# Both layers' attention of a two-layer diffusion backbone: one score buffer, one maximum and one exponential per head

## The chip, the cores and the metric

The kernel runs on one core of one Trainium2 chip. The metric is the device time of one execution in microseconds (us). Engines are named as in the profile: PE (TensorE matmul), PEld (its weight loads), DVE (VectorE), ACT (ScalarE), POOL (GpSimd), SP (SyncE, which issues most transfers).

## What is computed

Two layers over 1024 latent tokens and 256 context tokens, width 1024. Each layer mixes tokens (attention beside a gating or convolution branch), then sends them through 16 experts that choose their tokens by top-k. The change lies in the two attentions. Layer 0 has windows of 128 queries, each over up to 384 nearby keys and 256 context keys, 8 heads, with a sink; layer 1 is dense over 1024 + 256 = 1280 keys, 8 heads:

```python
def gqa_attend(q, k, v, mask, sink, scale):
    s = jnp.einsum('bqhgd,bkhd->bhgqk', q, k).astype(jnp.float32) * scale
    if mask is not None:
        s = jnp.where(mask, s, NEG_INF)
    if sink is not None:
        sk = jnp.broadcast_to(sink.astype(jnp.float32)[None, :, :, None, None], s.shape[:-1] + (1,))
        s = jnp.concatenate([s, sk], axis=-1)
    p = jax.nn.softmax(s, axis=-1)
    ...
    return jnp.einsum('bhgqk,bkhd->bqhgd', p.astype(v.dtype), v)

def dense_block_attention(q, k_all, v_all, scale):
    ...
    def block(nidx):
        qb = lax.dynamic_slice_in_dim(q, nidx * C_BLOCK, C_BLOCK, axis=1)
        return gqa_attend(qb[:, :, :, None], k_all, v_all, None, None, scale)[:, :, :, 0]
```

## The kernel before, in words

All matmuls take fp16 operands split into a high and a low part, so that a product is three matmuls (`mm3`, L141 to L143). Splitting a tile costs an ACT copy for the high part (L112) and a DVE subtraction for the low part (L114). Transposes of fp16 tiles go through DMA, issued on SP (`turn`, L147).

Work is written as streams (Python generators) that `weave` interleaves by weights. The scheduler of the framework then orders the instructions of each engine by priority, and each engine runs its list in that order. Attention's stream has a raised priority.

Layer 0 (`even`): 10 tiles of 128 tokens (2 context, 8 latent). `score(keep, u)` (L769) handles one latent head, or two context heads. It writes two score tiles `sps` of one PSUM bank each (up to 384 window keys, and 256 context keys; four banks in all, `MB[2]` = 4), takes the maximum of each (L791) and folds it into the negative maximum `negm` (L792), runs one exponential per head and block with its row sum (L799), splits the result and transposes it. `values()` multiplies with V one or two units later. The score of unit u+2 is written ahead of the values of unit u.

Layer 1 (`odd`): 8 tiles of 128 queries by 8 heads, in one sequence of 64 heads. `score(t, h, i)` (L1192) handles one of three key chunks of a head (`KB`: 512, 512 and 256 keys) in a score tile `sps1` of one bank, five banks in all (`AB[4]` = 5). Three matmuls per chunk (L1201) and one maximum (L1202). After the third chunk come the joint maximum (L1208), its scaling (L1209), three exponentials with row sums (L1218, each followed by a read of the accumulator), three splits into `ps1`, two DMA transposes (8 and 12 blocks of 128 columns, as high and low parts count apart) into `pT1`, and the sum of the three row sums (L1230). Scores run `LA` = 3 heads ahead of `values()`; `SP` says which chunks of head n+3 are scored with which of head n's value steps. Two of the eight banks serve the convolution and the projections (`zc`, `zt`), one the output accumulator `po1`.

Beside attention two streams fill PE in layer 1. First `conv_all` (576 matmuls of 512 columns into `cvps`), after which the output weights are scaled (`wraw`, L1159) and split (`owo`). Then `tails`: per tile 48 matmuls of the output projection (`yps`), a residual addition (`xx`, L301), router logits and affinities `aff` (L334). A top-k over the first 640 tokens (`tkvr`, L350 to L354) needs the first five tiles, a second over the other 384 (`tkvl`) the rest; then the expert stage starts and fills the remaining 596 us.

Of the kernel before, what the change touches and what calls it, by code (L numbers as in the profile page):

```python
# [47 lines left out]
GR = ((0,), (1, 2))  # L48
# [29 lines left out]
class Net:  # L78
# [554 lines left out]
    def even(self, xd, xdc, h2d, h2dc, then):  # L633
        nc, tc, V, S, T, G, Y, I = self.nc, self.tc, self.V, self.S, self.T, self.G, self.Y, self.I
        with self.pool("m0") as pm, self.pool("m0p", PSUM) as pp:
# [133 lines left out]
            def score(keep, u):  # L769

                qT, blocks, masks, W, nh = keep["q"], keep["blocks"], keep["masks"], keep["W"], keep["nh"]
                if u == 0:
                    keep["negm"] = self.small.tile([P, 8], F32, name="negm", bufs=2)
                    keep["den"] = self.small.tile([P, 8, 2], F32, name="den", bufs=2)
                    if len(blocks) == 1:
                        V.memset(keep["den"], 0.0)
                negm, hs = keep["negm"], slice(u * nh, u * nh + nh)
                pss, lim = [], nsink[:, hs]
                for first, n in blocks:
                    ps = pp.tile([P, 512], F32, name="sps", tag="s", bufs=MB[2])  # L780
                    pss.append(ps)
                    sl = slice(first * P, (first + n) * P)
                    for i in range(nh):
                        h, o = u * nh + i, ps[:, i * n * P:(i + 1) * n * P]
                        mk = masks if first == blocks[0][0] else []
                        T.matmul(o, qT[:, 0, h], kT[:, h // 4, sl], start=True, stop=False)
# [3 lines left out]
                    mx = self.small.tile([P, 2], F32, name="mx", bufs=4)  # L790
# [4 lines left out]
                c0 = 0  # L795
                for i in range(nh):
                    h = u * nh + i
                    for j, (_, n) in enumerate(blocks):
                        S.activation(pr[:, c0:c0 + n * P], pss[j][:, i * n * P:(i + 1) * n * P], AF.Exp, bias=negm[:, h:h + 1], scale=SC0,  # L799
                                     accum_out=keep["den"][:, h, j:j + 1])  # L800
                        c0 += n * P
# [7 lines left out]
            def values():  # L809
# [17 lines left out]
                V.tensor_tensor(es, den[:, :, 0], es, OP.add)  # L827
                V.tensor_tensor(es, den[:, :, 1], es, OP.add)
# [152 lines left out]
    def odd(self, ms, mw, xs, xsc, xd, h2d, W, then):  # L981
# [9 lines left out]
        if True:  # L991
# [109 lines left out]
            KB = ((0, 512), (512, 512), (1024, 256))  # L1101
            SP = ((), (0, 1), (2,))
# [6 lines left out]
            with self.pool("m1zp", PSUM) as pz:  # L1109
# [57 lines left out]
                if True:  # L1167
                    def Q(t):
                        qT = []
                        for i in range(2):  # L1170
# [5 lines left out]
                            S.activation(q, z, AF.Copy, scale=IS)  # L1176
# [14 lines left out]

                    def score(t, h, i):  # L1192

                        qT, (c0, w) = K[t][h // 4], KB[i]
                        if i == 0:
                            K["mx"] = self.small.tile([P, 3], F32, name="mx3", bufs=3)
                            K["sp"] = []
                        mx, sp = K["mx"], K["sp"]
                        ps = pp.tile([P, 512], F32, name="sps1", tag="s", bufs=AB[4])
# [6 lines left out]
                        dn = self.small.tile([P, 3], F32, name="dn3", bufs=3)  # L1206
                        nm = self.small.tile([P, 1], F32, name="nm1", bufs=3)
                        V.tensor_reduce(nm, mx, axis=AX.X, op=OP.max)  # L1208
                        V.tensor_scalar(nm, nm, -SC1, None, op0=OP.mult)  # L1209
                        pTs = []  # L1210
                        for g, parts in enumerate(GR):
                            n = sum(KB[i][1] for i in parts)
                            ps = pt1.tile([P, 2, n], F16, name="ps1", tag=f"ps{g}", bufs=AB[1])
                            o = 0
                            for i in parts:
                                w = KB[i][1]
                                pr = pt1.tile([P, 512], F32, name="pr1", bufs=AB[0])
                                S.activation(pr[:, :w], sp[i][:, :w], AF.Exp, bias=nm, scale=SC1, accum_out=dn[:, i:i + 1])  # L1218
                                self.split_a(pr[:, :w], ps[:, 0, o:o + w], ps[:, 1, o:o + w])
                                o += w  # L1220
                            pT = pt1.tile([P, 2, n // P, P], F16, name="pT1", tag=f"pT{g}", bufs=AB[2])
                            self.turn(pT.rearrange("p s b c -> p (s b) c"), ps.rearrange("p s c -> p (s c)"))
                            o = 0
                            for i in parts:
# [257 lines left out]
```

## Time and profile before

| | us |
|---|---|
| runs of the kernel, median of 3 (lowest to highest) | 2640.53 (2639.13 to 2646.84) |
| profiled execution, its own time | 2632.11 |
| span of its profile, first to last instruction | 2630.0 |
| busy in the span: PE / DVE / ACT | 2329.2 / 1997.7 / 1696.7 |
| layer 1's attention: first score matmul | 1503.4 |
| last convolution matmul | 1724.3 |
| last value matmul | 1937.20 |
| last output projection matmul | 1972.50 |
| mean granted TensorE clock (1.00 is 2.4 GHz) | 0.943 |

Times inside the program are counted from the first instruction of the profiled execution. Matmuls overlap in PE's pipeline, so a busy PE in a table of stretches need not be a full one; the distance between the starts of successive matmuls tells what one costs.

### The profile page before, as it was taken

Reading aid. Unit: us, or ns where it says so; the run is one execution under the profiler, and the core shown is the slowest. Engines: PE = TensorE matmul, PEld = TensorE weight load, DVE = VectorE, ACT = ScalarE, POOL = GpSimd, SP = SyncE. Lnnn points to the kernel's source line nnn. Section 1 sums busy time; section 2 is a strip of 40 time slices with the busy share of each in tenths; the row PEclk is TensorE's granted clock in tenths of the full one; section 3 lists DMA queues with packets and bytes.
Section 4 is the critical chain, followed back from the end, with each engine's and each line's share of the span. In section 5 each row is a group of like instructions: output and inputs, shape, how many; then the busy total and the mean of one; then the engine's idle time right before and its main releaser. Section 6 shows DMA issues by size and latency. Waiting matters only on the chain. (4 is left out here: it accounts for less than half of the span.)

```text
span 2630.0 us, 48132 instructions
## 1 busy us (share of the span) xinstructions
PE 2329.2 (89%) x19023; PEld 1415.0 (54%) x19023; DVE 1997.7 (76%) x3586; ACT 1696.7 (65%) x2748; POOL 320.6 (12%) x196
## 2 busy tenths in 40 slices
PE   6889998867999999999969999978982999999995
PEld 2335555543877778786836555535541444444442
DVE  5546767787887788777848687788796889888887
ACT  4434666535777787777726466567655777777774
POOL 1000000003111111111310000000025011112120
PEclk9999999877999999999989999989985999999998
DMA  8783555548998989888967577788866899999997
GB/s 321 192 213 84 134 104 116 123 126 312 352 337 324 328 328 325 327 320 300 326 187 203 119 143 143 133 151 184 176 175 272 311 364 395 368 360 367 361 363 274
DMA packets 461705, 660.25 MB, mean 251 GB/s; under 512 B 371083, under 2 KB 371387, under 8 KB 410789
## 3 DMA queue, kind: packets, MB, share of 16 engines
q1 hardware_dynamic: 439894, 582.81, 69.7%
q0 software_dynamic: 21584, 74.37, 9.8%
q8 instruction: 149, 2.44, 0.4%
q14 instruction: 78, 0.64, 0.1%
HBM read 525.82 MB, written 41.94 MB: 216 GB/s over the span
## 5 line engine op out<-in xcount | busy, mean ns | idle before, releaser
L101 DVE SCALAR_TENSOR_TENSOR spl<-raw,spl 128x2048 f16<-128x2048 f32 x369 | 834.6, 2285 | 167.3 <-ACT spl L100 166.5
L100 ACT ACTIVATE spl<-raw 128x2048 f16<-128x2048 f32 x369 | 693.5, 1911 | 166.4 <-DMA raw<-in_w 109.5
L141 PE MATMUL pa<-xsh,spl 128*128 128x160 f16 x1024 | 214.6, 233 | 2.3 <-ACT xsh L112 2.3
L143 PE MATMUL pb<-xsh,spl 128*128 128x160 f16 x1024 | 214.6, 233 | 0.5 <-DVE spl L101 0.5
L142 PE MATMUL pa<-xsl,spl 128*128 128x160 f16 x1024 | 214.7, 233 | 0.3 <-DVE xsl L114 0.3
L143 PE MATMUL pa<-xsh,spl 128*128 128x160 f16 x1024 | 214.7, 233 | 0.0
L142 PE MATMUL pb<-xsl,spl 128*128 128x160 f16 x1024 | 214.6, 233 | 0.0
L141 PE MATMUL pb<-xsh,spl 128*128 128x160 f16 x1024 | 214.5, 233 | 0.0
L141 PEld LDWEIGHTS <-spl 128*128 128x128 f16 x2048 | 200.6, 98 | 8.9 <-issue 8.0
L141 PE MATMUL y<-spl,gh 128*128 128x512 f16 x512 | 195.2, 384 | 9.0 <-ACT gh L112 8.4
L143 PEld LDWEIGHTS <-spl 128*128 128x128 f16 x2048 | 200.8, 98 | 1.1 <-DVE spl L101 0.7
L142 PEld LDWEIGHTS <-spl 128*128 128x128 f16 x2048 | 200.8, 98 | 0.3
L143 PE MATMUL y<-spl,gl 128*128 128x512 f16 x512 | 190.1, 386 | 11.4 <-DVE gl L114 11.3
L142 PE MATMUL y<-spl,gh 128*128 128x512 f16 x512 | 195.6, 382 | 1.8 <-DVE spl L101 1.8
L594 POOL DMA_INDIRECT xd<-ysb,idxl x31 | 113.2, 3652 | 532.3 <-DVE ysb L587 508.2
L1218 ACT ACTIVATE pr<-sps,nm 128x512 f32<-128x512 f32 (+1 forms) x192 | 116.7, 611 | 88.3 <-DVE nm L1209 67.7
L141 PE MATMUL po<-vS,pT 128*128 128x64 f16 x976 | 118.0, 198 | 49.1 <-DMA pT<-ps 32.5
L1201 PE MATMUL sps<-kT,qT 128*128 128x512 f16 (+1 forms) x576 | 134.4, 355 | 12.3 <-ACT pr L1218 11.9
L114 DVE TENSOR_TENSOR ps<-pr,ps 128x512 f16<-128x512 f32 (+1 forms) x192 | 112.2, 595 | 38.9 <-ACT ps L112 38.3
L141 PEld LDWEIGHTS <-pT 128*128 128x128 f16 x976 | 92.1, 101 | 82.8 <-DMA pT<-ps 46.5
L1202 DVE TENSOR_REDUCE mx<-sps 128x1 f32<-128x512 f32 (+1 forms) x192 | 112.8, 595 | 26.2 <-PE sps L1201 24.9
L208 PE MATMUL modps<-mslab,cs 128*2 128x512 f32 x384 | 88.5, 690 | 33.6 <-DMA mslab<-in_mod_w 28.7
(431 smaller groups left out, 5883.8 us busy)
## 6 DMA issues: line engine op xcount, KB each, us to landing
raw<-in_w SPq DMA_DIRECT2D x384, 1024.0 KB, 6.8
mslab<-in_mod_w SPq DMA_DIRECT2D x80, 512.0 KB, 4.8
mslab<-in_mod_w SPq DMA_DIRECT2D x8, 1024.0 KB, 8.2
raw<-in_wz SPq DMA_DIRECT2D x12, 512.0 KB, 6.4
raw<-in_wconv SPq DMA_DIRECT2D x24, 256.0 KB, 3.8
xin<-in_x POOLq DMA_DIRECT2D x8, 512.0 KB, 4.8
raw<-in_ev_wo SPq DMA_DIRECT2D x8, 512.0 KB, 6.9
xres<-in_x POOLq DMA_DIRECT2D x8, 512.0 KB, 5.4
```

Source lines behind the costliest of these rows:

```text
L100: self.S.activation(hi, raw, AF.Copy, scale=scale)
L101: self.V.scalar_tensor_tensor(lo, raw, scale, hi, op0=OP.mult, op1=OP.subtract)
L114: return self.V.tensor_tensor(lo, src, hi, OP.subtract)
L141: self.T.matmul(ps, lh, rh, start=first, stop=False)
L142: self.T.matmul(ps, lh, rl, start=False, stop=False)
L143: return self.T.matmul(ps, ll, rh, start=False, stop=last).ins
L208: T.matmul(ps[c0:c0 + 2], lhs, slab[:rows, g * 512:(g + 1) * 512], start=False, stop=(k == 8), tile_position=(0, c0))
L594: G.indirect_dma_start(out=xd, out_offset=IOA(ap=lat[0][:, e:e + 1], axis=0), in_=ysb, in_offset=None, compute_op=OP.add)
L1201: T.matmul(ps[:, :w], qT[:, 4 * j + h % 4], kT[:, k, c0:c0 + w], start=j == 0, stop=j == 2)
L1202: V.tensor_reduce(mx[:, i:i + 1], ps[:, :w], axis=AX.X, op=OP.max)
L1218: S.activation(pr[:, :w], sp[i][:, :w], AF.Exp, bias=nm, scale=SC1, accum_out=dn[:, i:i + 1])
```

## The change

In layer 0 a unit's blocks now lie side by side in one tile of two banks (two such tiles), placed so that the boundary between blocks falls on the bank boundary. One maximum, one folding step, and one exponential per head over all its keys (640 or 512) remain; the row sum needs no addition of two parts.

In layer 1 one tile `two` of five banks holds two heads, 1280 columns each, used in turn. The chunks of the odd half are 256, 512 and 512 keys so that each stays within a bank. One maximum (negated), one exponential over 1280 keys with the whole row sum, one split, and two transposes of 10 blocks each remain. The scale `SC1` moves into the copy of q. The buffer `pr1` of the exponentials is one tile of 1280 (before, two of 512).

```diff
-                for first, n in blocks:
-                    ps = pp.tile([P, 512], F32, name="sps", tag="s", bufs=MB[2])
...
+                ps = pp.tile([P, 1024], F32, name="sps", tag="s", bufs=MB[2] // 2)
+                base = 512 - blocks[0][1] * P if len(blocks) > 1 else 0
...
-                    V.tensor_reduce(mx[:, :nh], ps[:, :nh * n * P].rearrange("p (h w) -> p h w", h=nh), axis=AX.X, op=OP.max)
-                    V.scalar_tensor_tensor(negm[:, hs], mx[:, :nh], -SC0, lim, op0=OP.mult, op1=OP.min)
-                    lim = negm[:, hs]
+                V.tensor_reduce(mx[:, :nh], ps[:, base:base + nh * W].rearrange("p (h w) -> p h w", h=nh), axis=AX.X, op=OP.max)
+                V.scalar_tensor_tensor(negm[:, hs], mx[:, :nh], -SC0, nsink[:, hs], op0=OP.mult, op1=OP.min)
...
+                    S.activation(pr[:, i * W:i * W + W], ps[:, base + i * W:base + i * W + W], AF.Exp, bias=negm[:, h:h + 1], scale=SC0,
+                                 accum_out=keep["den"][:, h:h + 1])
...
-            KB = ((0, 512), (512, 512), (1024, 256))
-            SP = ((), (0, 1), (2,))
+            KB = ((0, 512), (512, 512), (1024, 256)), ((0, 256), (256, 512), (768, 512))
+            SP = (0, 1), (2,)
...
-                            S.activation(q, z, AF.Copy, scale=IS)
+                            S.activation(q, z, AF.Copy, scale=IS * SC1)
...
+                    two = pp.tile([P, 2560], F32, name="sps1")
+
                     def score(t, h, i):
...
+                        n = (8 * t + h) % 2
+                        qT, (c0, w) = K[t][h // 4], KB[n][i]
+                        ps = two[:, 1280 * n:1280 * n + 1280]
                         for j, k in enumerate((h, h, 8)):
-                            T.matmul(ps[:, :w], qT[:, 4 * j + h % 4], kT[:, k, c0:c0 + w], start=j == 0, stop=j == 2)
-                        V.tensor_reduce(mx[:, i:i + 1], ps[:, :w], axis=AX.X, op=OP.max)
-                        sp.append(ps)
-                        if i < len(KB) - 1:
+                            T.matmul(ps[:, c0:c0 + w], qT[:, 4 * j + h % 4], kT[:, k, c0:c0 + w], start=j == 0, stop=j == 2)
+                        if i < len(KB[n]) - 1:
                             return
...
+                        V.tensor_reduce(nm, ps, axis=AX.X, op=OP.max, negate=True)
...
+                        pr = pt1.tile([P, 1280], F32, name="pr1", bufs=1)
+                        S.activation(pr, ps, AF.Exp, bias=nm, accum_out=K["rd", t][:, h:h + 1])
+                        pf = pt1.tile([P, 2, 2, 640], F16, name="ps1", bufs=AB[1])
+                        prg = pr.rearrange("p (g c) -> p g c", g=2)
+                        self.split_a(prg, pf[:, :, 0], pf[:, :, 1])
...
-                        for b in range(w // P):
-                            vb, vs = c0 // P + b, slice(h * 64, h * 64 + 64)
+                        for b in range(5):
+                            vb, vs = 5 * i + b, slice(h * 64, h * 64 + 64)
```

How the order of instructions moves is shown at three places. The first is PE's list at layer 1's second head (`sps` is a score tile, `kT` and `qT` the keys and queries, `wc` convolution weights; a wait names the engine whose semaphore it awaits). Before, the head's first two chunks:

```order
L1201 LDWEIGHTS qT_18993
L1201 MATMUL sps_19060<-kT_16901,qT_18993 128x512
L1201 LDWEIGHTS qT_18993
L1201 MATMUL sps_19060<-kT_16901,qT_18993 128x512
L1201 LDWEIGHTS qT_18993
L1201 MATMUL sps_19060<-kT_16901,qT_18993 128x512
L1201 LDWEIGHTS qT_18993
L1201 MATMUL sps_19065<-kT_16901,qT_18993 128x512
L1201 LDWEIGHTS qT_18993
L1201 MATMUL sps_19065<-kT_16901,qT_18993 128x512
```

Of the change, the same head's first chunk, with the convolution ahead of it:

```order
L141 LDWEIGHTS wc
L141 MATMUL cvps<-hTl,wc 128x512
L142 LDWEIGHTS wc
L142 MATMUL cvps<-hTl,wc 128x512
L1193 LDWEIGHTS qT_18662
L1193 MATMUL sps_18639<-kT_16569,qT_18662 128x256 [waits Activation_49]
L1193 LDWEIGHTS qT_18662
L1193 MATMUL sps_18639<-kT_16569,qT_18662 128x256
```

The chunks had tiles of their own and no wait; now every head's matmuls name one tile, and the head's first one waits for ACT.

The second place is DVE's list near the end of layer 1's attention (`mx` and `nm` come from the maximum over scores, `ps<-pr` is the subtraction that gives the low part). Before:

```order
L1202 TENSOR_REDUCE mx_24516<-sps_24517 128x1
L114 TENSOR_TENSOR ps_24473<-pr_24474,ps_24473 128x512
L1202 TENSOR_REDUCE mx_24516<-sps_24522 128x1
L1202 TENSOR_REDUCE mx_24516<-sps_24545 128x1
L114 TENSOR_TENSOR ps_24480<-pr_24481,ps_24480 128x512
L1202 TENSOR_REDUCE mx_24606<-sps_24607 128x1
L1208 TENSOR_REDUCE nm_24551<-mx_24516 128x1
L1230 TENSOR_REDUCE rd<-dn_24469 128x1
L1249 TENSOR_TENSOR oc<-po_23773,rd 128x512
L114 TENSOR_TENSOR ps_24480<-pr_24485,ps_24480 128x256
```

Of the change, four heads there:

```order
L113 TENSOR_TENSOR ps_22944<-pr_22942,ps_22944 128x2x640
L1197 TENSOR_REDUCE nm_22990<-sps_18639 128x1
L113 TENSOR_TENSOR ps_22994<-pr_22992,ps_22994 128x2x640
L1197 TENSOR_REDUCE nm_23049<-sps_18639 128x1
L113 TENSOR_TENSOR ps_23053<-pr_23051,ps_23053 128x2x640
L1197 TENSOR_REDUCE nm_23099<-sps_18639 128x1
```

Chunks of neighbouring heads stood mixed; now a head's subtraction and the next head's maximum alternate strictly.

The third place is DVE's list where the first top-k of layer 1 stands (`tkvr`, `tkir`; `oc` is the last step of the attention of a tile, here of the last one). Before, in the midst of that top-k:

```order
L354 MATCH_REPLACE aff<-tkvr,aff 16x640
L350 MAX tkvr<-aff 16x8
L1249 TENSOR_TENSOR oc<-po_24593,rd 128x512
L352 MAX_INDEX tkir<-tkvr,aff 16x8
L114 TENSOR_TENSOR oh<-oc,oh 128x512
L354 MATCH_REPLACE aff<-tkvr,aff 16x640
```

Of the change, the start of that top-k, 26 rows behind the last `oc`:

```order
L126 TENSOR_SCALAR rstdt<-rstt,rsyt 128x1
L300 SCALAR_TENSOR_TENSOR xx<-yps,xx 128x512
L333 COPY aff<-affps 16x128
L349 MAX tkvr<-aff 16x8
L351 MAX_INDEX tkir<-tkvr,aff 16x8
L353 MATCH_REPLACE aff<-tkvr,aff 16x640
```

It had begun before the attention ended; now it begins after the fifth tile's affinities, which come behind the attention.

## Rows read from the trace of the kernel before

**Rows 1.** Stretches of layer 1: length, PE, PEld, DVE, ACT, POOL busy, clock, DMA.

```profile
1503.00:1725.00 222.00, 215.69 (x1850) 118.25 (x1849) 168.75 (x424) 140.72 (x351) 0.00 (x0) 1.00 0.73 136
1725.00:1784.00 59.00, 38.70 (x381) 21.22 (x379) 52.76 (x113) 42.03 (x95) 0.00 (x0) 0.80 0.81 172
1784.00:1855.00 71.00, 62.81 (x603) 37.10 (x599) 54.95 (x153) 49.12 (x122) 2.14 (x4) 1.00 0.89 170
1855.00:1918.00 63.00, 58.96 (x574) 36.22 (x574) 46.46 (x133) 44.62 (x112) 2.66 (x5) 1.00 0.87 178
1918.00:1937.00 19.00, 10.79 (x142) 8.16 (x142) 16.87 (x46) 10.50 (x28) 0.53 (x1) 0.72 1.00 188
1937.00:1973.00 36.00, 36.00 (x184) 18.08 (x182) 35.04 (x87) 20.46 (x19) 17.56 (x7) 0.96 0.45 171
```

**Rows 2.** Groups by line and shape, 1500 to 1940 us: count, busy us, mean ns, idle before.

```profile
L1202 DVE TENSOR_REDUCE mx<-sps 128x1 f32<-128x512 f32 x128 | 87.2, 684 | 15.6 <-PE sps L1201 14.6
L1218 ACT ACTIVATE pr<-sps,nm 128x512 f32<-128x512 f32 x128 | 86.5, 680 | 70.0 <-DVE nm L1209 67.7 <-DVE ps L114 2.0
L114 DVE TENSOR_TENSOR ps<-pr,ps 128x512 f16<-128x512 f32 x128 | 85.7, 684 | 35.9 <-ACT ps L112 35.6
...
L112 ACT ACTIVATE ps<-pr 128x512 f16<-128x512 f32 x128 | 75.1, 625 | 0.3
...
L1218 ACT ACTIVATION_READ_ACCUMULATOR pr<-sps,nm 128x1 f32 x192 | 37.6, 196 | 0.0
...
L1218 ACT ACTIVATE pr<-sps,nm 128x256 f32<-128x256 f32 x64 | 30.1, 471 | 18.3 <-DVE ps L114 18.3
L1202 DVE TENSOR_REDUCE mx<-sps 128x1 f32<-128x256 f32 x64 | 26.7, 417 | 10.6 <-PE sps L1201 10.3
L114 DVE TENSOR_TENSOR ps<-pr,ps 128x256 f16<-128x256 f32 x64 | 26.6, 416 | 3.0 <-ACT ps L112 2.7
L112 ACT ACTIVATE ps<-pr 128x256 f16<-128x256 f32 x64 | 26.6, 415 | 1.7
...
L1159 DVE TENSOR_TENSOR wraw<-wraw,m2b 128x1024 f32<-128x1024 f32 x8 | 9.5, 1215 | 1.2 <-DMA wraw<-in_od_wo 1.2
...
L101 DVE SCALAR_TENSOR_TENSOR owo<-wraw,owo 128x1024 f16<-128x1024 f32 x8 | 9.4, 1208 | 0.0
```

**Rows 3.** PE's timeline: start us, duration us; value matmuls, then convolution matmuls.

```profile
1517.16 0.19 PE L142 MATMUL po<-vS,pT 128*128 128x64 f16 x1
1517.19 0.19 PE L143 MATMUL po<-vS,pT 128*128 128x64 f16 x1
...
1625.45 0.38 PE L141 MATMUL cvps<-hTl,wc 128*128 128x512 f16 x1
1625.67 0.38 PE L142 MATMUL cvps<-hTl,wc 128*128 128x512 f16 x1
```

**Rows 4.** Layer 0: PE's wait, 190 to 400 us; exponentials, 190 to 570 us.

```profile
PE sps L786 <- ACT pr L799: 7.6, 5, 3.1
...
L799 ACT ACTIVATE pr<-sps,negm 128x256 f32<-128x256 f32 x80 | 37.1, 467 | 7.7 <-DVE negm L792 6.1 <-DVE p L114 1.6
...
L799 ACT ACTIVATE pr<-sps,negm 128x384 f32<-128x384 f32 x48 | 27.5, 574 | 12.0 <-DVE negm L792 7.1 <-DVE p L114 4.8
```

**Rows 5.** Timelines of DVE and of ACT: one handover between them.

```profile
1625.73 0.14 DVE L1209 TENSOR_SCALAR nm<-nm 128x1 f32<-128x1 f32 x1
...
1625.91 0.69 ACT L1218 ACTIVATE pr<-sps,nm 128x512 f32<-128x512 f32 x1 [1.68 <-DVE nm L1209]
```

**Rows 6.** Transposes into `pT1`, 1500 to 1940 us, from issue to landing.

```profile
DMA to landing us min/median/max: 3.0/3.7/6.3
```

**Rows 7.** DVE's timeline: the first top-k's first and last step, the second's first.

```profile
1925.35 0.82 DVE L350 MAX8 tkvr<-aff 16x8 f32<-16x640 f32 x1
...
1974.39 0.23 DVE L360 TENSOR_SCALAR tkir<-tkir 16x128 f32<-16x128 uint32 x1
...
1997.64 0.55 DVE L350 MAX8 tkvl<-aff 16x8 f32<-16x384 f32 x1
```

More of the change, by code (lines that the diff above doesn't have):

```diff
@@ L773, in score @@
                     keep["negm"] = self.small.tile([P, 8], F32, name="negm", bufs=2)
-                    keep["den"] = self.small.tile([P, 8, 2], F32, name="den", bufs=2)
-                    if len(blocks) == 1:
-                        V.memset(keep["den"], 0.0)
+                    keep["den"] = self.small.tile([P, 8], F32, name="den", bufs=2)
                 negm, hs = keep["negm"], slice(u * nh, u * nh + nh)
-                pss, lim = [], nsink[:, hs]
-                for first, n in blocks:
-                    ps = pp.tile([P, 512], F32, name="sps", tag="s", bufs=MB[2])
[L781 to L784, printed above, removed]
+                ps = pp.tile([P, 1024], F32, name="sps", tag="s", bufs=MB[2] // 2)
+                base = 512 - blocks[0][1] * P if len(blocks) > 1 else 0
+                for i in range(nh):
+                    h, c0 = u * nh + i, base + i * W
+                    for first, n in blocks:
+                        o = ps[:, c0:c0 + n * P]
+                        c0 += n * P
                         mk = masks if first == blocks[0][0] else []
+                        sl = slice(first * P, (first + n) * P)
                         T.matmul(o, qT[:, 0, h], kT[:, h // 4, sl], start=True, stop=False)
@@ L789, in score @@
                             T.matmul(o[:, c:c + P], identb, maskb[:, w], start=False, stop=j == len(mk) - 1)
[L790 to L793 removed]
+                mx = self.small.tile([P, 2], F32, name="mx", bufs=4)
+                V.tensor_reduce(mx[:, :nh], ps[:, base:base + nh * W].rearrange("p (h w) -> p h w", h=nh), axis=AX.X, op=OP.max)
+                V.scalar_tensor_tensor(negm[:, hs], mx[:, :nh], -SC0, nsink[:, hs], op0=OP.mult, op1=OP.min)
                 pr = pm.tile([P, 640], F32, name="pr", bufs=MB[3])
[L795 removed]
                 for i in range(nh):
                     h = u * nh + i
[L798 to L801, printed above, removed]
+                    S.activation(pr[:, i * W:i * W + W], ps[:, base + i * W:base + i * W + W], AF.Exp, bias=negm[:, h:h + 1], scale=SC0,
+                                 accum_out=keep["den"][:, h:h + 1])
                 n = nh * W
@@ L1205, in score @@
                             return
-                        dn = self.small.tile([P, 3], F32, name="dn3", bufs=3)
                         nm = self.small.tile([P, 1], F32, name="nm1", bufs=3)
[L1208 to L1224, printed above, removed]
-                                w = KB[i][1] // P
-                                pTs.append(pT[:, :, o:o + w])
-                                o += w
@@ L1231, in score @@
+                        prg = pr.rearrange("p (g c) -> p g c", g=2)
+                        self.split_a(prg, pf[:, :, 0], pf[:, :, 1])
+                        pTs = []
+                        for g in range(2):
+                            pT = pt1.tile([P, 2, 5, P], F16, name="pT1", tag=f"pT{g}", bufs=AB[2])
+                            self.turn(pT.rearrange("p s b c -> p (s b) c"), pf[:, g].rearrange("p s c -> p (s c)"))
+                            pTs.append(pT)
                         K["p", t, h] = pTs
@@ L1261, in att_all @@
                             pTs = K.pop(("p", t, h))
-                            for i in range(len(KB)):
+                            for i in range(2):
                                 pend.append((t, h, i, pTs[i]))
```

14 lines of the change are left out of this document (2 added, 12 removed).

## The prediction

> **What bounds the kernel now.** I read first the busy time by stretch of layer 1's attention [rows 1], since most of the change lies there, and then what each of its instructions costs [rows 2]. Call a head's pieces S (9 score matmuls), M (maximum), E (exponential), C (high part, ScalarE), D (low part, VectorE), T (two DMA transposes) and V (30 value matmuls). In the first stretch, 222 us for heads 0 to 33, PE is busy 215.69 us at clock 1.00. That it is also full follows from spacing: 512-column matmuls start 0.215 us apart and value matmuls 0.03 us [rows 3]. So S takes 6 x 0.215 + 3 x 0.11 = 1.6 us, V 0.9, nine projections of q (384 columns) 1.45. By the built order this stretch holds 552 convolution matmuls (118.7 us), 34 heads of S and V (85) and 14 such projections (20): 224 us. Nothing taken from VectorE or ScalarE shortens it. In the second stretch (59 us, heads 33 to 42) PE is busy 38.70 us at clock 0.80 and VectorE 52.76: VectorE paces it. In the third and fourth (heads 42 to 63) PE is at 62.81 of 71 and 58.96 of 63, because output projections fill it; then the last heads drain until 1937, where the last value matmul stands, and the three remaining output tiles take 36 us, 12 us each. Layer 0 is close to PE-bound too; what the scores there wait for is the exponential of an earlier head, 7.6 us in five waits between 190 and 400 us [rows 4].
>
> **What the change saves.** Per element and fixed part follow from the two widths of [rows 2]. M: 684 and 417 ns, so 1280 keys take 684 + 768 x 1.043 = 1.49 us where 2 x 684 + 417 = 1.79 stood. D: 684 and 416, the same, 1.49. E: 680 and 471, so 1.31 us where 1.83 stood. C: 625 and 415, so 1.26 where 1.67 stood. An accumulator read costs 196 ns and two of three go. Over 64 heads VectorE loses 38 us in M and D and some 28 us in three small instructions a head, taken at 0.145 us like the one of the three in [rows 5], ScalarE 33 + 26 + 25 = 84 us. No row shows a 1280-wide access over several banks; the nearest, at 512, has no term that grows with it, so I take the straight line and keep +0.3 us each for M and E as the upper bound.
>
> **What the change adds in layer 1.** Both halves of the new score buffer are one tile. In the built order the first matmul of head 1's S waits for ScalarE, where before two whole chunks of head 1 went ahead without that wait. Counted through the built program, the value awaited is that of the exponential of the head just before, for head 1 and for all later ones, although the halves alternate. So S(n+1) starts only after E(n): two buffers in name, one in effect. Queued behind the waiting S on PE are V, convolution and output projections.
>
> Here the Trainium skill, PSUM — Partial Sum Buffer, section "PSUM bank collisions raise a hardware error", bears: it says to guard PSUM by bank and not by address, and that two engines on one bank collide. 1280 columns are two and a half banks of 512, so by that rule the halves share the middle bank and only that third of S must wait. The built order makes all of S wait, also where an even head begins in a bank that the odd half never touches; I go by the order, and the rival below prices the rule.
>
> VectorE's order now reads D(n), M(n+1), D(n+1), with little else between, where before chunks of two heads alternated. The loop is therefore E 1.31, 0.1 for the rest of its accumulator read [rows 2], C 1.26, D 1.49, M 1.49 and two handovers of 0.04 [rows 5]: 5.7 us a head at best. S(n+1) lies beside C and D (2.8 us) only if PE is free within 0.9 us of E(n). V(n) is ready at E(n) + 2.8 + 3.7 (landing of a transpose [rows 6]) = 6.5 us, its second half about 1.4 later.
>
> I walked PE's order by these numbers.
> - **Heads 0 to 33.** From head 2 to 18 each head brings 21 convolution matmuls (4.5 us) and PE stays full: 128 us after a start of 15. From head 18 the convolution is thinner and stands in the wrong places: the waits for E(n-1) before S(20), S(28), S(31), S(32) come to 3.65, 3.7, 1.15 and 3.85 us, those for transposes before V(17), V(20), V(28), V(29) to 2.3, 0.95, 2.5 and 1.7. S(33) starts 98 us after S(18). Sum 15 + 128 + 98 = 241 against 222: **+20** (bounds +10 and +32; below, if landings come at 3.0, above, if conversions on ScalarE fall between E and C).
> - **Heads 33 to 42.** Eight scalings and eight low parts of the output weights, 1.2 us each [rows 2], now stand between M and D or between D and M, where the loop waits for them: four heads take 37 us instead of 23, the other five 30. 67 against 59: **+8** (0 to +12).
> - **Heads 42 to 53.** The order packs 3.5 tiles of output projection here: 168 matmuls (36 us), S and V (27.5), q (3), transposes and router (11), with 5 us of waits: 83 against 71, **+12** (+5 to +15).
> - **Heads 53 to the end.** Nothing fills PE. S(n+2) stands behind the first half of V(n), so two heads take 2.8 + 3.7 + 0.45 + 1.8 + 1.5 + 1.45 = 11.7 us, and one 5.9. Ten heads are 59 us, the last drain 14, slower clock 3: 76 against 63 + 19: **-6** (-10 to +6).
>
> So the attention ends 34 us later. Four output tiles, not three, then remain (192 of 384 matmuls in the order, 144 before), 12 us more on PE. But top-k over the first 640 tokens needs tile 4, which is now among the four: by the order its first instruction stands behind some 2.6 tiles, 31 us after the attention. Before it ran from 1925.35 to 1974.39, 49 us among tail work, and the last top-k began at 1997.64, 60.6 us after 1937 [rows 7]. Now the first one ends at 31 + 49 = 80: **+20** instead of 12 (bounds +12, +30). Transposes stay two a head, 10 blocks each instead of 8 and 12: nothing on SP's queue (bound: the landings' spread, 3.0 to 6.3 us, in the walk already). The scale moved into q's copy costs nothing, the same instruction.
>
> **Layer 0.** Here tiles stay separate, two of two banks, and the order hardly moves. Per head E drops from 574 + 467 ns with two reads to 574 + 256 x 0.836 = 788 with one [rows 4], 0.45 us with the read, VectorE by about 0.3. PE's waits on the exponential, 7.6 us in these 210 and about as much again later, lose perhaps half, and VectorE's dense last stretch a few us: **-8** (0 to -18).
>
> **Sum.** 20 + 8 + 12 - 6 + 20 - 8 = +46. The profiled execution took 2632.11 us around a span of 2630.0, 0.3% below the median 2640.53; against the median 2687 us.
>
> **The rivals.**
> - **Faster (0.07).** The 150 us taken off two engines shows. For: VectorE paces heads 33 to 42, and 5.7 us a head is below the 6.3 to 6.6 of the last three stretches. Against: 222 us are PE's, and the loop crosses three engines in series. It wins if the waits before S fall where PE has work, so that heads 42 to 63 go at 5.9: 21 x 5.9 + 14 = 138 against 153, -15; first stretch +3, second and end 0, layer 0 -15: 2613. It decides once E(n) to E(n+1) stays under PE's own demand of 6.4 us.
> - **No change (0.04).** Layer 0 gives back what layer 1 loses; it needs every lower bound at once, about 2640.
> - **Shared bank only (0.17).** If S meets just the conflict over the middle bank, the 12 us of waits before S in the first stretch go and tile 4 is early enough for top-k (+12, not +20): 46 - 12 - 8 = +26, 2667. Milder bounds in the walk end here too; the order speaks against it. The section of the Trainium skill named above, PSUM — Partial Sum Buffer, would have it so.
> - **Worse (0.20).** With PE idle the clock falls: between 1918 and 1937, with PE at 10.79 of 19 us, it was granted at 0.72 [rows 1]. At half speed S takes 3.2 us and two heads nearly 14, so +11 at the end and +5 around head 38; interposed work on ScalarE adds 9: 2712. Wide reads dearer by 0.3 us each would add as much.
> - **The forecast (0.52)**, 2687, within 2670 to 2705.
>
> **How the numbers follow.** Reaching 2655 to 2722 takes in the milder and the worse case and the bounds of the walk, and leaves out the 0.11 of faster or equal and the far end of worse. About 0.3%, 8 us, is what a measurement here can tell from no change: faster 0.07, same 0.04, slower 0.89.
>
> **What would show it.** Right: in layer 1, PE's S waits for E in nearly every head after 18; VectorE and ScalarE lose some 66 and 84 us of busy time and yet idle more; the attention lasts near 468 us instead of 434; the last ten heads show PE half busy at a low clock; the first top-k runs after the attention. Wrong: S starting before the previous E ends, a loop under 5.5 us, or an attention of 440 us or less. The step most likely to fail is the first stretch, since ScalarE's and VectorE's other work is only roughly placed there.

## The result, and the profile after

| | before | after |
|---|---|---|
| median, us (lowest to highest) | 2640.81 (2639.13 to 2646.84) | 2718.17 (2708.59 to 2723.66) |
| profiled execution, its own time | 2632.11 | 2723.66 |
| layer 1: first score matmul | 1503.4 | 1507.7 |
| last convolution matmul | 1724.3 | 1765.4 |
| last value matmul | 1937.2 | 2003.5 |
| last output projection matmul | 1972.5 | 2052.3 |
| first expert matmul (`pa`) | 2039.1 | 2131.5 |

The change is slower: ratio 1.0285, 95% interval 1.0251 to 1.0319. The medians lie 77 us apart and the two profiled executions 91.5, since that of before lies below all of its timed runs and that of after is the slowest of its own. The 91.5 us divide into 4.3 ahead of layer 1's attention, 62 in it (434.0 to 496.1, from the first score matmul to the end of the last value matmul; the table gives starts), 26 from there to the first expert matmul (101.7 to 127.7), and nothing behind. The 62 come although 48 output projection matmuls fewer lie in that stretch.

The table of stretches, cut at the same heads (0 to 33, 33 to 42, 42 to 53, 53 to the last value matmul, then the output projections); columns as in [rows 1]:

```profile
1507.70:1765.80 258.10, 227.09 (x1885) 123.03 (x1886) 157.41 (x209) 120.93 (x166) 0.00 (x0) 0.97 0.63 119
1765.80:1837.80 72.00, 44.69 (x404) 24.97 (x401) 52.20 (x54) 37.02 (x46) 0.00 (x0) 0.79 0.72 156
1837.80:1922.70 84.90, 79.48 (x696) 47.85 (x693) 49.84 (x85) 42.59 (x61) 3.22 (x6) 0.96 0.77 162
1922.70:2003.80 81.10, 48.47 (x504) 30.09 (x501) 38.65 (x41) 33.75 (x42) 1.07 (x2) 0.78 0.61 121
2003.80:2052.50 48.70, 47.59 (x241) 24.15 (x240) 26.12 (x68) 25.23 (x26) 18.89 (x9) 0.98 0.58 212
```

Against [rows 1] the first stretch has opened: 31 of its 258 us are PE's idle time, where 6 of 222 were. The fourth, which output projections had filled, has PE busy for 48 of 81 us at clock 0.78. In [rows 1] the stretches end at round times; between exactly the same heads, the four of before are:

```profile
1503.40:1725.20 221.80, 215.67 (x1850) 118.43 (x1851) 168.69 (x424) 140.52 (x350) 0.00 (x0) 1.00 0.73 136
1725.20:1787.30 62.10, 39.73 (x385) 21.57 (x383) 56.06 (x119) 44.43 (x101) 0.00 (x0) 0.81 0.80 169
1787.30:1861.00 73.70, 67.49 (x636) 39.62 (x636) 54.72 (x154) 49.99 (x126) 2.14 (x4) 1.00 0.93 176
1861.00:1937.40 76.40, 64.23 (x681) 41.72 (x679) 60.25 (x170) 51.66 (x130) 3.19 (x6) 0.93 0.88 177
```

The instructions of layer 1, by line and shape, 1500 to 2005 us; columns as in [rows 2]:

```profile
L113 DVE TENSOR_TENSOR ps<-pr,ps 128x1280 f16<-128x1280 f32 x64 | 95.4, 1491 | 77.7 <-ACT ps L111 76.9
L1197 DVE TENSOR_REDUCE nm<-sps 128x1 f32<-128x1280 f32 x64 | 95.2, 1487 | 46.4 <-PE sps L1193 46.2
L1201 ACT ACTIVATE pr<-sps,nm 128x1280 f32<-128x1280 f32 x64 | 84.9, 1327 | 193.7 <-DVE nm L1197 189.5 <-DVE ps L113 2.1 <-DVE mst L121 1.9
L111 ACT ACTIVATE ps<-pr 128x1280 f16<-128x1280 f32 x64 | 81.0, 1266 | 1.2
...
L1201 ACT ACTIVATION_READ_ACCUMULATOR pr<-sps,nm 128x1 f32 x64 | 12.3, 193 | 0.0
```

Each wide instruction costs what the straight line through [rows 2] gave (1.49, 1.49, 1.31 and 1.26 us): reading two and a half banks at once adds at most 20 ns. The saved work is real, and ScalarE spends it waiting: 189.5 us for the maximum, where the exponentials of before waited 67.7 for theirs [rows 2].

Waits of layer 1's attention in after, longest first, without those of POOL (engine, line, what ended the wait; us in total, times, longest):

```profile
...
ACT pr L1201 <- DVE nm L1197: 189.5, 54, 7.3
...
DVE ps L113 <- ACT ps L111: 76.9, 44, 3.2
PE po L140 <- DMA pT<-ps: 71.9, 38, 7.9
DVE nm L1197 <- PE sps L1193: 46.2, 32, 3.8
...
PE sps L1193 <- ACT pr L1201: 20.0, 14, 3.5
```

And two rows of PE's waits in before, for the same stretch:

```profile
PE po L141 <- DMA pT<-ps: 32.5, 31, 3.0
PE sps L1201 <- ACT pr L1218: 11.9, 11, 4.1
```

The chain goes once around: exponential waits for maximum, maximum for scores, scores for the previous exponential or for the queue in front of them. On PE the longer wait is not the one before scores (+8 us) but the one before value matmuls, for transposes (+39), and the next scores stand behind those. The last heads show it. Timelines of DVE, of ACT and of PE, three cuts (start, duration, in brackets the idle time before and what ended it):

```profile
1955.62 1.49 DVE L113 TENSOR_TENSOR ps<-pr,ps 128x1280 f16<-128x1280 f32 x1 [0.47 <-ACT ps L111]
1957.81 1.49 DVE L1197 TENSOR_REDUCE nm<-sps 128x1 f32<-128x1280 f32 x1 [0.69 <-PE sps L1193]
1962.15 1.49 DVE L113 TENSOR_TENSOR ps<-pr,ps 128x1280 f16<-128x1280 f32 x1 [2.85 <-ACT ps L111]
1965.21 1.49 DVE L1197 TENSOR_REDUCE nm<-sps 128x1 f32<-128x1280 f32 x1 [1.58 <-PE sps L1193]
...
1959.39 1.33 ACT L1201 ACTIVATE pr<-sps,nm 128x1280 f32<-128x1280 f32 x1 [3.80 <-DVE nm L1197]
1966.80 1.33 ACT L1201 ACTIVATE pr<-sps,nm 128x1280 f32<-128x1280 f32 x1 [4.69 <-DVE nm L1197]
1972.54 1.33 ACT L1201 ACTIVATE pr<-sps,nm 128x1280 f32<-128x1280 f32 x1 [3.02 <-DVE nm L1197]
...
1961.66 0.24 PE L140 MATMUL po<-vS,pT 128*128 128x64 f16 x1 [3.45 <-DMA pT<-ps]
1962.45 2.72 PE L1193 MATMUL sps<-kT,qT 128*128 128x256 f16 x9
1967.20 0.20 PE L140 MATMUL po<-vS,pT 128*128 128x64 f16 x1 [1.58 <-DMA pT<-ps]
1968.27 1.78 PE L1193 MATMUL sps<-kT,qT 128*128 128x512 f16 x9 [0.46 <-ACT pr L1201]
```

The subtraction of one head ends at 1957.1; its first transpose lets the value matmuls go at 1961.66, and only behind them come the scores at 1962.45, although their exponential had ended at 1960.72. They take 2.72 us, at a granted clock of 0.65; then come the maximum and the exponential (1966.80), 7.4 us after the last one. The next exponential follows 5.7 us later: those scores (1968.27) wait for the exponential itself, and lie beside copy and subtraction. Two heads take 13.15 us here, and 12.5 to 14.3 from head 53 on.

The order that the prediction read from the built program shows in every head of the trace: a head's first score matmul starts at the earliest 0.14 us after the end of the exponential of the head before, in all 63 cases. Before, it started 1.4 to 13.5 us ahead of the end of that head's last exponential (median 6.4). Head 58's first scores and head 57's last exponential of before:

```profile
1894.03 0.81 PE L1201 MATMUL sps<-kT,qT 128*128 128x512 f16 x3
...
1896.70 0.46 ACT L1218 ACTIVATE pr<-sps,nm 128x256 f32<-128x256 f32 x1
```

The first top-k, which before began at 1925.35 [rows 7], 12 us ahead of the last value matmul, begins at 2037.4, 34 us behind it. One row of the view by tile, with first and last start:

```profile
L349 DVE MAX8 tkvr<-aff x8: 805/816/817, 2037.4 to 2059.0; 16x8 f32<-16x640 f32 x8
```

### The profile page after: what moved, and what is told of

It reads as the page before. It is cut to its first block, busy times and chain, and to the rows that moved or that the text cites. A ratio compares the mean times of both kernels' runs of the same rounds, so it can differ in the third digit from the quotient of the medians.

```text
span 2721.9 us, 46946 instructions
## 1 busy us (share of the span) xinstructions
PE 2358.4 (87%) x19023; PEld 1430.6 (53%) x19023; DVE 1965.8 (72%) x2998; ACT 1631.0 (60%) x2236; POOL 312.4 (11%) x196
## 5 line engine op out<-in xcount | busy, mean ns | idle before, releaser
L142 PE MATMUL y<-spl,gl 128*128 128x512 f16 x512 | 189.5, 384 | 17.0 <-DVE gl L113 16.9
L1201 ACT ACTIVATE pr<-sps,nm 128x1280 f32<-128x1280 f32 x64 | 84.9, 1327 | 193.7 <-DVE nm L1197 189.5
L140 PE MATMUL po<-vS,pT 128*128 128x64 f16 x976 | 116.2, 199 | 83.0 <-DMA pT<-ps 71.9
L593 POOL DMA_INDIRECT xd<-ysb,idxl x31 | 107.0, 3451 | 553.4 <-DVE ysb L586 529.1
L113 DVE TENSOR_TENSOR ps<-pr,ps 128x1280 f16<-128x1280 f32 x64 | 95.4, 1491 | 77.7 <-ACT ps L111 76.9
L1197 DVE TENSOR_REDUCE nm<-sps 128x1 f32<-128x1280 f32 x64 | 95.2, 1487 | 46.4 <-PE sps L1193 46.2
```

The source lines that it names most:

```text
L113: return self.V.tensor_tensor(lo, src, hi, OP.subtract)
L140: self.T.matmul(ps, lh, rh, start=first, stop=False)
L142: return self.T.matmul(ps, ll, rh, start=False, stop=last).ins
L593: G.indirect_dma_start(out=xd, out_offset=IOA(ap=lat[0][:, e:e + 1], axis=0), in_=ysb, in_offset=None, compute_op=OP.add)
L1197: V.tensor_reduce(nm, ps, axis=AX.X, op=OP.max, negate=True)
L1201: S.activation(pr, ps, AF.Exp, bias=nm, accum_out=K["rd", t][:, h:h + 1])
```

## The experiments

The theory was the prediction's (below: one-tile theory): because both halves of the score buffer are one tile, a head's scores start only after the exponential of the head before, and the late transposes follow from that. The waits of the profile suggest a rival (late transposes): a head's first transpose now stands behind a copy and a subtraction of the whole head, and PE waits for it whatever the score tiles are. A second rival is the buffer `pr1` of the exponentials, one tile now, which the next head's exponential can't write before this head's subtraction has read it. A third question is where the 26 us behind the attention come from.

Ratios stand against the kernel before on the same chip, with 95% intervals. "Attention" is layer 1's, from the first score matmul to the end of the last value matmul in the one profile of the run (434.0 before, 496.1 after), "end" the time from there to the first expert matmul (101.7 and 127.7). What one profile can tell: the runs with one layer changed have the instructions of layer 1 in the same order as before and as after, and differ from them by 2.7 and 0.9 us in the attention and by about 1 in the end.

**Layer 0 alone, layer 1 alone.** Each takes the hunks of one layer.

> The change in layer 0 alone, layer 1 as before. The prediction's term was -8 us (0 to -18): near 2633. The trace of the changed kernel speaks for less: its expert stage of layer 0 starts 0.5 us earlier than before, so 2640, no difference that can be measured. Rival: layer 0's gain is real and lost behind it (2633 or less here).

Measured: 2625.08 us, ratio 0.9932 (0.9907 to 0.9956), where 2640 was expected; the rival was right. The profile of after had misled here. With one and the same order of layer 0, that trace reached the expert stage at 645.3 us, and the nine other runs that carry the change at 633.1 to 640.2 (mean of all ten 638.0); the three with the old layer 0 at 645.8, 648.4 and 652.8 (mean 649.0). So layer 0 gains about 11 us up to there.

> The change in layer 1 alone, layer 0 as before. If the whole loss is layer 1's, 2718 (2712 to 2722), and attention from first score matmul to last value matmul takes 496 us. By the prediction's terms for layer 1 (20 + 8 + 12 - 6 + 20 = 54) it would be 2695.

Measured: 2724.39 us, ratio 1.0313 (1.0278 to 1.0347), attention 495.2, end 127.0. The whole loss is layer 1's. This loss less layer 0's gain is 83 - 17 = 66 us, where the change as a whole lost 77; the intervals overlap.

**Chunk tiles.** The score buffer and its instructions as before, the rest of the change kept:

```diff
-                    two = pp.tile([P, 2560], F32, name="sps1")
+                        ps = pp.tile([P, 512], F32, name="sps1", tag="s", bufs=AB[4])
+                        V.tensor_reduce(mx[:, i:i + 1], ps[:, :w], axis=AX.X, op=OP.max)
...
+                        V.tensor_reduce(nm, mx, axis=AX.X, op=OP.max, negate=True)
...
-                        S.activation(pr, ps, AF.Exp, bias=nm, accum_out=K["rd", t][:, h:h + 1])
+                        for g, (o, n) in enumerate(KB):
+                            S.activation(pr[:, o:o + n], sp[g][:, :n], AF.Exp, bias=nm, accum_out=dn[:, g:g + 1])
+                        V.tensor_reduce(K["rd", t][:, h:h + 1], dn, axis=AX.X, op=OP.add)
```

> The changed kernel, but layer 1's scores in five one-bank tiles, a maximum and an exponential per chunk, as before; one wide high copy, one wide subtraction and two transposes of ten blocks a head stay as in the change. One-tile theory (the next head's scores wait for this head's exponential, and all else follows): attention at most 445 us, PE's waits for transposes back near 33 us, 2640 to 2655. Late-transposes rival (the first transpose of a head is issued only after the whole head is split, and the value matmuls wait for it): waits for transposes stay near 72 us, attention 480 or more, 2700 or more.

Measured: 2637.23 us, no difference from before that can be told (ratio 0.9986, 0.9966 to 1.0006), 3 us below the range; attention 425.3, end 127.0. PE's waits in the attention:

```profile
PE po L140 <- DMA pT<-ps: 27.1, 30, 3.1
PE sps L1194 <- ACT pr L1206: 10.6, 14, 3.8
```

One-tile theory: with the chunk tiles the waits for transposes fall from 71.9 to 27.1 us although a head is still split whole and its transposes issued after that. The attention ends up 9 us shorter than before, with the 48 output matmuls (some 12 us) still missing from it; the end keeps its 25 us loss, which therefore has another cause. `pr1` stays one tile in this run, so that it isn't what cost the 62 us.

**Half splits.** The change with its one tile, high copy and subtraction in halves:

```diff
-                        self.split_a(prg, pf[:, :, 0], pf[:, :, 1])
...
                         for g in range(2):
+                            self.split_a(prg[:, g], pf[:, g, 0], pf[:, g, 1])
```

> The changed kernel, with the high copy and the subtraction in two halves of 640 keys, each followed by its transpose. One-tile theory: exponential, copies, subtractions and next maximum stay in series; the first subtraction starts 0.6 us earlier, so the loop shortens by at most 0.6 us a head on some 30 heads that it paces, less the fixed part of two more instructions: 2700 to 2718. Late-transposes rival: the first half's transpose is issued some 1.4 us earlier in every head, and half of the 72 us of waits before value matmuls goes: 2680 or less.

Measured: 2688.12 us, ratio 1.0167 (1.0131 to 1.0204); attention 465.0, waits for transposes 59.7 us. Half of the attention's loss goes, more than the one-tile theory gave (2700 at the least), less than the rival. Earlier transposes do help where scores are queued behind value matmuls. Where two delays stand in one loop, shortening either of them helps: this run does not say which comes first.

**The share of the streams.** Why does one output tile more stay behind the attention, in after and with chunk tiles? The streams are interleaved by the counts that they yield. A head counted 3 x 0.6 for score chunks and 3 x 0.3 for value steps, 2.7; with two value steps it counts 2.4, and the attention runs ahead of the output projection.

```diff
                                     values()
-                                    yield 0.3
+                                    yield 0.45
```

> The changed kernel, with the share of the attention stream against the output projection restored: a value step of layer 1 counts 0.45 in the weave instead of 0.3, so that a head counts 2.7 as before (three value steps of 0.3 and three score steps of 0.6) and not 2.4. In the built order 144 output projection matmuls then stand behind the last value matmul, as before, and not 192, and the first top-k starts ahead of the last attention step. Weave theory (the post-attention loss of 26 us comes from this count alone): last value matmul to first expert matmul falls from 128 to about 103 us, 2690 to 2700. Rival (those 48 matmuls only move into the attention and lengthen it by their 12 us, and the late top-k comes from the slow attention): 2708 or more.

Measured: 2683.93 us, ratio 1.0143 (1.0126 to 1.0159), 6 us below the range; end 99.6, attention 496.9. The 48 output matmuls moved into a PE that was idle, and the attention did not grow; the first top-k begins 55 us before its end. The end's loss in the change is this count, and has nothing to do with PSUM: the score buffer is the change's own.

**Only a third shared.** 1024 keys of a head in a tile of two banks, two of them in turn; the other 256 in half of one bank that both heads share as one tile; two maxima and two exponentials a head:

```diff
-                    two = pp.tile([P, 2560], F32, name="sps1")
+                    rest = pp.tile([P, 512], F32, name="sps2")
...
+                            K["s"] = pp.tile([P, 1024], F32, name="sps1", tag="s", bufs=2)
+                        big, small = K["s"], rest[:, 256 * n:256 * n + 256]
...
+                        V.tensor_reduce(mx[:, 0:1], big, axis=AX.X, op=OP.max)
+                        V.tensor_reduce(mx[:, 1:2], small, axis=AX.X, op=OP.max)
+                        V.tensor_reduce(nm, mx, axis=AX.X, op=OP.max, negate=True)
...
+                        S.activation(pr[:, 1024:], small, AF.Exp, bias=nm, accum_out=dn[:, 1:2])
+                        S.activation(pr[:, :1024], big, AF.Exp, bias=nm, accum_out=dn[:, 0:1])
```

> The changed kernel, but a head's scores in a tile of two banks for 1024 keys (two such tiles) and half of one shared bank for the other 256, so two maxima and two exponentials a head; the shared bank is one tile, so only a third of a head's score matmuls waits for the exponential of the head before, and that exponential comes first. One-tile theory: attention 450 us or less, and since four output tiles still remain, 2640 to 2665. Rival (the wide copy and subtraction in series are what paces a head, whatever the score tiles): attention 475 or more, 2690 or more.

Measured: 2616.24 us, ratio 0.9889 (0.9874 to 0.9905), below the range of either theory; attention 404.0, end 128.1. PE's waits:

```profile
PE po L140 <- DMA pT<-ps: 21.2, 25, 2.3
PE sps L1196 <- ACT pr L1208: 10.1, 5, 3.8
PE sps L1196 <- ACT pr L1209: 0.9, 2, 0.6
```

The maxima cost more than the one of after (1.22 + 0.42 + 0.15 us a head instead of 1.49), and the wide copy and subtraction are the same. What is gone is only that a head's scores wait for the head before as a whole: two thirds of them wait 0.9 us in all, the third in the shared bank 10.1. What takes longer now is the wait for `pr1`, 23.0 us until the subtraction has read it (2.1 in after):

```profile
L1208 ACT ACTIVATE pr<-sps,nm 128x256 f32<-128x256 f32 x64 | 30.2, 471 | 94.8 <-DVE nm L1204 71.6 <-DVE ps L113 23.0 <-DVE mst L121 0.2
```

This attention too holds 48 output matmuls fewer than that of before; the run with 0.45 below holds as many.

**Both repairs.** Chunk tiles with the 0.45:

> Both repairs together: scores in five one-bank tiles as before (the run of chunk tiles, 2637) and the restored weave share. If the 25 us behind the attention and the 36 us in it are separate losses, 2610 to 2620, less than before and than layer 0 alone (2625). Rival (the moved matmuls lengthen the attention by as much as they shorten the end): 2630 to 2640.

Measured: 2617.16 us, ratio 0.9895 (0.9879 to 0.9910); attention 420.6, end 102.0. The two losses are separate, and with as many output matmuls in it as before the attention is 13 us shorter.

**Three banks.** The kernel before with `AB[4]` = 3 for 5, nothing else:

> The kernel before with three score tiles of one bank in layer 1 instead of five, so that each chunk's score matmuls wait for an exponential of the head before; instructions stay narrow. One-tile theory (buffers decide, not widths): attention 470 us or more, 2670 or more. Rival (the widths, or the whole-head split, decide): within 10 us of 2641.

Measured: 2746.89 us, ratio 1.0383 (1.0368 to 1.0399); attention 547.3, end 98.1, PE's waits for transposes 92.1 us and for exponentials 16.8. Fewer buffers with narrow instructions give the same picture as the change and a larger loss, and again the wait shows before the value matmuls, not before the scores.

**Shared third and restored share.** The run above with a third shared, with 0.45, with halves on top, and with 0.6:

> The run with the shared rest (two tiles of two banks and one shared bank; 2616) with the restored weave share (a value step counts 0.45). In the built order 144 output projection matmuls stand behind the last value matmul instead of 192, but the first top-k still starts behind the last attention step. If the end's loss is the fourth output tile and the late top-k in about equal parts: 12 us less, 2600 to 2608. Rival (the late top-k alone sets the end, and it stays late): 2612 or more.

> The run above, with high copy and subtraction in two halves, each followed by its transpose. With separate score tiles PE waits only 21 us for transposes in layer 1's attention, so the halves have little left to give: within 8 us of the run above. Rival (the whole-head split was a second loss of its own, worth 30 us as in the run of half splits): 15 us or more below the run above.

> The run with the shared rest and a value step that counts 0.6: 96 output projection matmuls stand behind the last value matmul, and the first top-k starts just ahead of the last attention step in the built order. If the end is what the share decides, last value matmul to first expert matmul falls to 90 us or less and the attention grows by at most 15 us: 2585 to 2600. Rival (the attention takes the moved matmuls one for one): within 5 us of the run with 0.45.

| | median us | ratio (95%) | attention | end | output matmuls behind the attention |
|---|---|---|---|---|---|
| 0.45 | 2606.16 | 0.9854 (0.9834 to 0.9874) | 410.2 | 110.6 | 144 |
| 0.45, halves | 2626.28 | 0.9926 (0.9906 to 0.9946) | 410.7 | 124.4 | 168 |
| 0.6 | 2617.29 | 0.9895 (0.9866 to 0.9924) | 427.2 | 89.4 | 96 |

With 0.45 this is the fastest kernel of the study, and within its range. The end is 110.6 and not 102: its first top-k still begins 20 us behind the attention. Its stretches, cut at the same heads as above:

```profile
1496.10:1595.40 99.30, 95.00 (x855) 53.54 (x856) 77.75 (x145) 64.20 (x115) 0.00 (x0) 1.00 0.84 146
1595.40:1689.90 94.50, 91.02 (x865) 51.52 (x862) 77.41 (x141) 57.76 (x105) 0.00 (x0) 1.00 0.83 149
1689.90:1740.00 50.10, 49.91 (x478) 28.59 (x477) 38.24 (x69) 30.49 (x55) 0.00 (x0) 1.00 0.86 161
1740.00:1811.20 71.20, 53.61 (x510) 30.86 (x507) 60.98 (x92) 44.41 (x74) 0.00 (x0) 0.86 0.85 175
1811.20:1906.30 95.10, 89.11 (x828) 54.42 (x827) 60.03 (x137) 52.78 (x97) 4.27 (x8) 0.96 0.83 172
```

(The first stretch is shown in two, at head 18.) Up to head 42 PE is busy for 236 of 244 us, at clock 1.00 (with 540 of the attention's 552 convolution matmuls, all of which before were done by head 33). Halves gain nothing in the attention once the scores don't wait, and were expected not to; that the run is 20 us slower was expected by neither theory. Its end is 13.8 us longer, with 24 output matmuls more behind the attention and the first top-k 10 us further behind it; its layer 1 begins 7 us later, which is no more than that start varies (1491 to 1508 us in the ten profiles with the new layer 0). Why the halves reorder the tail is open. The run with 0.6 missed its range (2585 to 2600) and its rival's too: the end is the shortest, but the attention takes 17 of the 21 us back, and the expert stage behind takes 601 instead of 587 us; why, is open.

## Why the prediction was right, and where its sizes were off

The sign and the cause held: one tile for two heads puts exponential, copy, subtraction and maximum of successive heads in series, and giving scores their own tiles brings the attention from 496 to 425 us (chunk tiles) or 404 (a third shared). The sum was +46 where the medians say +77: 2718 lies outside the 2670 to 2705 of the forecast itself, beside the 2712 of the "worse" rival, and near the upper end of the range. By its terms:

- **Heads 0 to 33**, forecast +20 (bounds +10 and +32), measured 258.1 against 221.8, **+36**, above its upper bound. This is the step that was named as the likeliest to fail, and it did, by size: the walk had too few waits for transposes. From head 0 to 18 the forecast had PE full (143 us; measured 147.7, with 7.0 us of waits, nearly all for transposes). From 18 to 33 (110.4 us, forecast 98) the waits for exponentials were 9.8 us where 12.35 were forecast, those for transposes 13.1 instead of 7.45. Of the 36 us, PE's idle time makes 25; most of the rest is the clock, which the walk took as full: 0.99 was granted up to head 18 and 0.94 from there to head 33, 1.00 before [rows 1], which on 141 and 86 busy us is some 7. The stretch also holds one more group of nine q projections, 1.45 us.
- **Heads 33 to 42**, +8: **+10**. **Heads 42 to 53**, +12: **+11**. The lengths themselves were forecast as 67 and 83 us and measured as 72.0 and 84.9; the differences fit better, since the prediction's stretches of before (59 and 71) ended at round times, where the heads take 62.1 and 73.7.
- **Heads 53 to the end**, -6 (-10 to +6): **+5**. Half of this miss is the baseline: head 53 of before begins at 1861 and not 1855, so that 76.4 us and not 82 stood against the 76 forecast. The other half, 81.1 for 76, is the loop. In the pair of heads above, 13.15 us instead of 11.7, scores were priced at full speed and took 2.72 us, 0.9 more; from the end of the subtraction to the first value matmul it was 4.5 us and not 3.7. The "worse" rival had named this clock and said nearly 14 us for two heads, which is about what they take.
- **Behind the attention**, +20: **+26**. The fourth tile and the late top-k were read rightly from the built order (the first top-k ends 81 us after the attention, 80 was forecast). The second top-k, which then begins 21 us later than before, takes 30.4 us from its first to its last step instead of 24.6; why, is open. What was not seen is where the order comes from: the "shared bank only" rival lets the top-k be early as soon as PE's waits go. The run with the restored share shows that it follows from the count of two value steps for three; undoing it cost the attention nothing there (496.9 for 496.1).
- **Layer 0**, -8 (0 to -18): **-17** by the medians of the run of layer 0 alone (interval -12 to -25), 11 of it before the expert stage. Its mechanism was wrong. PE's waits for the exponential were to halve from the 7.6 us of [rows 4]; in the same window of after the row reads

```profile
PE sps L784 <- ACT pr L794: 12.2, 5, 3.3
```

More, not less (a score tile is freed as a whole by one longer exponential, which would explain it; that was not tried by itself). It is no accident of one profile. From 90 us to the expert stage this wait takes 17.1 to 17.8 us in the three profiles with the old layer 0 and 20.1 to 23.8 in the ten with the new one, while that for transposes takes 14.1 to 16.1 and 7.0 to 10.8, that for the output's transpose (`oT`) 6.0 and 3.3 to 4.8. PE's idle time up to the expert stage falls by 8 us on average. So the gain came by waits that the prediction had not priced; that shorter work on VectorE and ScalarE brings the transposes earlier would explain it, and was not tried by itself.

The saving was sized well as a sum of durations. In layer 1 M and D lose 36 us (38 forecast), the three small instructions that go 28 (28), the exponentials 32 (33), the high copies 21 (26), the accumulator reads 25 (25). As busy time it was sized too high: over the whole span, with layer 0's savings in it, VectorE is busy 32 us less (66 forecast for layer 1 alone) and ScalarE 66 (84). The records of successive instructions overlap, as three of VectorE before show:

```profile
1893.16 0.27 DVE L126 TENSOR_SCALAR rstt<-rsyt,mst 128x1 f32<-128x1 f32 x1
1893.35 0.15 DVE L1230 TENSOR_REDUCE rd<-dn 128x1 f32<-128x3 f32 x1
1893.41 0.42 DVE L114 TENSOR_TENSOR ps<-pr,ps 128x256 f16<-128x256 f32 x1
```

The small one lasts 0.15 us and takes 0.06 from its start to the next. Summed, the durations of VectorE fall by 78 us and those of ScalarE by 112. With 588 and 512 instructions fewer, 46 us of overlap go on each engine, 0.08 and 0.09 us for each instruction.

"S waits for E in nearly every head" was right in the order and wrong as a sign in the trace. PE stood there only 14 times; it stood 38 times, in 29 heads, at value matmuls ahead of them in its list. The scores at 1962.45, whose exponential was done at 1960.72, show it: the wait is booked on the first instruction of PE's list that is late, not on the one whose buffer is short. The Trainium skill, PSUM — Partial Sum Buffer, section "Engine vs sequencer instructions", says that matmuls start and complete in program order. These rows agree with it.

The rival "shared bank only" (+26, 2667) did not occur in this change. The run with a third shared comes near its construction, and takes 2616 with the fourth tile still behind. The Trainium skill, PSUM — Partial Sum Buffer, section "PSUM bank collisions raise a hardware error", asks for a guard by bank. That run keeps to it, since the shared bank is one tile; PE's waits for the exponential behind it are the 10.1 us above, no more than the 11.9 of before. In the change itself a guard by bank would have left more waits than the rival says: odd heads write their 256 columns in the shared bank first (their first chunk in the order shown with the change), so that in PE's list their other two chunks would stand behind it. No run has that guard.

## What to carry to other kernels

Before several buffers are put into one tile to make instructions wider, count the waits in the built program: where the tile is tracked as one, two halves are one buffer, and with 113 us less of the wide instructions on VectorE and ScalarE in layer 1 its attention became 62 us longer. Tiles that end at a buffer's border (two of two banks, one shared remainder) kept most of the width and the overlap: with the same output matmuls in it (the run with 0.45) the attention is 24 us shorter than before. And where streams are interleaved by counts, a step that is merged or split needs its count corrected: two value steps for three cost some 26 us at a place that the change never touched.

## What the runs showed that was not expected

- One exponential, one maximum, one copy and one subtraction over 1280 columns take 1327, 1487, 1266 and 1491 ns, the straight line from 256 and 512 columns within 20 ns. The first two read two and a half banks in one instruction, at no extra cost beyond that.
- The instructions that went freed less of their engine than they had lasted, by 0.08 us each on VectorE and 0.09 on ScalarE. That is about half of a small one (0.145 and 0.196 us).
- Transposes of ten blocks land no later than those of eight and twelve. The row of after (that of before is [rows 6]):

```profile
DMA to landing us min/median/max: 3.4/3.6/5.4
```

- Layer 0, with one and the same order of instructions, took between 633.1 and 645.3 us to the expert stage in ten profiled executions. A difference of 10 us in one stage, read from one profile on each side, is no result.
